# A Gated DeltaNet head's output norm moved out of its recurrence, one head later

## The chip, the cores and the metric

The kernel runs on one core of a Trainium2 chip. The core has a matrix engine (TensorE, PE in the rows), a vector engine (VectorE, DVE), an activation engine (ScalarE, ACT), GpSimd (POOL) and a sync engine (SP), which here issues the DMA transfers. Each engine runs its own list of instructions in order; semaphores tie the lists together. The metric is device time in microseconds (us) of one execution, the median over runs.

## The reference

One decoder block: half a SwiGLU feed-forward step (FFN1), then two mixers side by side (gated linear attention, GLA, and Gated DeltaNet with 8 heads), their gated merge, a second feed-forward step (FFN2) and a final norm. Sequence 1024, model width 1024, float32. The change sits in the Gated DeltaNet heads, whose core is

```python
def gated_delta_attention(q, k, v, g, beta):      # chunks of 64, heads of 128
    ...
    kk = jnp.einsum("bhnid,bhnjd->bhnij", k_beta, k) * decay
    M = jnp.eye(CHUNK, dtype=f32) + jnp.where(strict, kk, 0.0)
    sol = lax.linalg.triangular_solve(M, rhs, left_side=True, lower=True, unit_diagonal=True)
    ...
    def step(S, xs):                               # the recurrence over chunks
        qdc, qkc, uc, wc, kc, gc = xs
        v_new = uc - jnp.einsum("bhcd,bhdv->bhcv", wc, S)
        o = jnp.einsum("bhcd,bhdv->bhcv", qdc, S) + jnp.einsum("bhij,bhjv->bhiv", qkc, v_new)
        S = S * gc[..., None, None] + jnp.einsum("bhcd,bhcv->bhdv", kc, v_new)
        return S, o

def head_rms_norm(o, w, heads):                    # the norm that the change moves
    oh = o.reshape(b, t, heads, -1)
    oh = oh * lax.rsqrt(jnp.mean(oh * oh, axis=-1, keepdims=True) + EPS) * w.astype(jnp.float32)
```

## The kernel before, in words

The time runs through FFN1 (until about 735 us), the eight delta heads (735 to 1395), GLA (to about 1880), the output product, and FFN2. The order of instructions on each engine is not written out by hand. The program is emitted head by head; when it is built, a scheduler places every instruction on its engine's list by its own estimate of when inputs and buffers are ready, so a change in one place can move others. On the chip each list then runs strictly in that order.

One turn `i` of the loop over heads (L1236 and below) emits parts of three heads: the preparation of head `i+1` (`delta_prep`), V projection, levels and recurrence of head `i` (`delta_v`, `delta_levels`, `delta_rec`), and K and Q projections of head `i+2`. All projections are the L138 matmuls: a float32 weight is brought by DMA into `raw` (L112), cast to `wh` by ACT (L119) and its rest taken as `wl` by DVE (L120); these two stand in a scheduler priority block, which lets them be placed far ahead of the code around them. `raw` has two buffers.

`delta_prep` of the next head: transposes of K on PE (L876, into two PSUM banks), squares on ACT (L880, tiles `jk`) and products on DVE (L882) that read those two banks, a Newton iteration for the row norms on DVE (L884 to L889), q·k and k·k products on PE (L902, four banks, each read by DVE in L904 and, with the Newton result, in L908). The result `em` goes to DRAM (`l_d`, L914) and back in another layout (`lt`, L917). POOL then inverts it in 31 steps (L924, L927), and SP writes the inverse to DRAM (`x_d`, L932 and L933, eight transfers) and reads it back (`xb`, `yb`, L944 and L945). The levels (L981, L994 on PE with copies L985, L995 on ACT and subtractions L987, L989, L996 on DVE) finish the inverse `yi`, and the recurrence (PE L1014, L1018, L1022, L1024, L1027; DVE L1016, L1020, L1032) uses it. The loop over heads is therefore also a loop through DMA and POOL: a preparation must pass through `l_d`, `lt`, the inversion and `x_d` before the next head's levels.

The recurrence collects 512 columns of output in a PSUM bank `qo`. The pool of these banks (`bank()`) has four. After each half the norm follows at once: ACT squares `qo` (L1037), DVE adds (L1038), PE sums over the partitions with a matrix of ones (L800, into another bank), ACT takes Ln (L802) and Exp (L803), each with a load of its table, and a square (L804), DVE L805 (which reads the sum's bank), L806, and L1040, which reads `qo`. The two banks stay taken until L805 and L1040.

Of the kernel before, what the change touches and what calls it, by code (L numbers as in the profile page):

```python
# [10 lines left out]
AF = mybir.ActivationFunctionType  # L11
ALU = mybir.AluOpType
# [3 lines left out]
P = 128  # L16
# [5 lines left out]
EPS = 1e-6  # L22
# [16 lines left out]
ORDER = (0, 2, 4, 6, 1, 3, 5, 7)  # L39
# [697 lines left out]
def mixer(st, sto, tc, pool, start, xs, load_unit, dense, ptile, bank, rsqrt_newton, split, new_x, accumulate,  # L737
          ounits, dram, pr, ident, ones, cst, eye, wlr, win, wout, y_d, h_d, sqrt_table, strassen_products, wp, psum, divide, recent, pinned, run):
    nc = tc.nc
# [9 lines left out]
    def big(tag, bufs=None, shape=None):  # L749
        p = cur[0] if cur else me if tag in early else mb  # L750
        return p.tile(shape or [P, T], F32, name=tag, tag=tag, bufs=bufs)
# [8 lines left out]
    def v3(t, n=NCH):  # L760
        return t.rearrange("p (n i) -> p n i", n=n)

    ph = mp.tile([P, 99], F32, name="ph")
# [12 lines left out]
    def half():  # L776
        return sp.tile([P, 512], F32, name="h", tag="h", bufs=4)
# [20 lines left out]
    def out_rms(sq):  # L798
        q = bank()
        nc.tensor.matmul(out=q, lhsT=ones, rhs=sq, start=True, stop=True)  # L800
        t, y = half(), half()
        nc.scalar.activation(out=t, in_=q, func=AF.Ln)  # L802
        nc.scalar.activation(out=y, in_=t, func=AF.Exp, scale=-0.5)  # L803
        nc.scalar.activation(out=t, in_=y, func=AF.Square)  # L804
        nc.vector.scalar_tensor_tensor(out=t, in0=q, scalar=-0.5, in1=t, op0=ALU.mult, op1=ALU.mult)  # L805
        nc.vector.scalar_tensor_tensor(out=y, in0=t, scalar=1.5, in1=y, op0=ALU.add, op1=ALU.mult)  # L806
        return y
# [13 lines left out]
    def delta_kq(i, a, kq=None, steps=None):  # L821
        h = ORDER[i]
        kq = kq or big(f"kq{i % 3}", 1, [P, NCH, 2, P])

        def put(a):
            def f(hf, acc, sg):
                nc.vector.scalar_tensor_tensor(out=kq[:, hf * 4:hf * 4 + 4, a, :], in0=q4(sg), scalar=1.0,
                                               in1=q4(acc), op0=ALU.add, op1=ALU.mult)
            return f

        if a:
            conv_silu(U_DQ + h, h * 4, put(1))
        else:
            conv_silu(U_DK + h, (8 + h) * 4, put(0), (6,), steps)
        return kq

    def delta_decay(i):
        h = ORDER[i]
        gb = big("gb", 2)
        nc.sync.dma_start(out=gb, in_=g_d[h:h + 1, :].broadcast_to([P, T]))  # L840
        gb4 = gb.rearrange("p (n a i) -> p n a i", n=NCH, a=2)
        gla, glb = gb4[:, :, 0, 63], gb4[:, :, 1, 63]
        db = sp.tile([P, NCH, 2], F32, name="db", tag="db", bufs=2)
        nc.vector.tensor_copy(out=db, in_=ngt[:, h, :].unsqueeze(2).broadcast_to([P, NCH, 2]))
        nc.vector.tensor_add(out=db[0:64, :, 1], in0=db[0:64, :, 1], in1=gla[0:64])
        kdec = sp.tile([P, NCH], F32, name="kdec", tag="kdec", bufs=2)
        nc.vector.tensor_add(out=kdec, in0=db[:, :, 1], in1=glb)
        nc.scalar.activation(out=kdec, in_=kdec, func=AF.Exp)
        gl = sp.tile([P, NCH], F32, name="glast", tag="glast", bufs=2)
        nc.vector.tensor_add(out=gl, in0=gla, in1=glb)  # L850
        nc.scalar.activation(out=gl, in_=gl, func=AF.Exp)
        em = big("em", 1)
        nc.vector.tensor_tensor(out=em.rearrange("p (m i) -> p m i", i=64),
                                in0=gb.rearrange("p (m i) -> p m i", i=64),
                                in1=db.rearrange("p n a -> p (n a)").unsqueeze(2).broadcast_to([P, 16, 64]),
                                op=ALU.add)
        nc.vector.tensor_tensor(out=v3(em), in0=v3(em), in1=minmask.unsqueeze(1).broadcast_to([P, NCH, P]),
                                op=ALU.min)
        nc.scalar.activation(out=em, in_=em, func=AF.Exp)
        gla_c = sp.tile([P, NCH], F32, name="glac", tag="glac", bufs=2)  # L860
        nc.vector.tensor_copy(out=gla_c, in_=gla)
        nc.vector.tensor_tensor(out=gb4[:, :, 1, :], in0=gb4[:, :, 1, :],
                                in1=gla_c.unsqueeze(2).broadcast_to([P, NCH, 64]), op=ALU.add)
        nc.scalar.activation(out=gb, in_=gb, func=AF.Exp)

        return gb, gl, kdec, em
# [133 lines left out]
    def delta_rec(kq, qsq, vt3, gl, kst, qk, cj, yi):  # L1000
        kT, qT = kq[:, :, 0, :], kq[:, :, 1, :]
        yi3, kst3, qk3 = v3(yi), v3(kst), v3(qk)
        S = None
        oT = big("oT", 3)
        for b in range(2):
            qo = bank()
            for n in range(4):
                c = b * 4 + n
                rw = sp.tile([P, 256], F32, name="rw", tag="Sg", bufs=2)
                if S is None:  # L1010
                    r = vt3[:, c, :]
                else:
                    q = bank()
                    nc.tensor.matmul(out=q[:, :P], lhsT=kT[:, c, :], rhs=S, start=True, stop=True)  # L1014
                    r = rw[:, :P]
                    nc.vector.tensor_sub(out=r, in0=vt3[:, c, :], in1=q[:, :P])  # L1016
                q = bank()
                nc.tensor.matmul(out=q[:, :P], lhsT=yi3[:, c, :], rhs=r, start=True, stop=True)  # L1018
                w = rw[:, P:]
                nc.vector.tensor_scalar(out=w, in0=q[:, :P], scalar1=cj[:, c:c + 1], scalar2=None, op0=ALU.mult)  # L1020
                oc = qo[:, n * P:(n + 1) * P]
                nc.tensor.matmul(out=oc, lhsT=w, rhs=qk3[:, c, :], start=True, stop=(S is None))  # L1022
                if S is not None:
                    nc.tensor.matmul(out=oc, lhsT=S, rhs=qT[:, c, :], start=False, stop=True)  # L1024
                if c < NCH - 1:
                    q = bank()
                    nc.tensor.matmul(out=q[:, :P], lhsT=kst3[:, c, :], rhs=w, start=True, stop=True)  # L1027
                    s2 = sp.tile([P, P], F32, name="S", tag="S", bufs=2)
                    if S is None:
                        nc.vector.tensor_copy(out=s2, in_=q[:, :P])  # L1030
                    else:
                        nc.vector.scalar_tensor_tensor(out=s2, in0=S, scalar=gl[:, c:c + 1], in1=q[:, :P],  # L1032
                                                       op0=ALU.mult, op1=ALU.add)
                    S = s2
            cc = slice(b * 512, b * 512 + 512)
            osq = half()
            nc.scalar.activation(out=osq, in_=qo, func=AF.Square, scale=P ** -0.5)  # L1037
            nc.vector.scalar_tensor_tensor(out=osq, in0=osq, scalar=EPS * EPS, in1=qsq[:, cc], op0=ALU.add, op1=ALU.add)  # L1038
            fac = out_rms(osq)
            nc.vector.scalar_tensor_tensor(out=oT[:, cc], in0=qo, scalar=ph[:, 98:99], in1=fac,  # L1040
                                           op0=ALU.mult, op1=ALU.mult)
        return oT

    def gla_pre(h):
        la = big("la")
# [179 lines left out]
    for b in range(2):  # L1225
        q = bank()
# [17 lines left out]
    outs = []  # L1244
    for i in range(8):
        kq, (x_d, kst, qk, cj, rs), gl0 = kqs[i], preps[i], gl
        gb0 = gb
        prep = None
        if i < 7:
            gb, gl, kdec, em = nd  # L1250
            prep = delta_prep(i + 1, kqs[i + 1], kdec, em, preps)
            next(prep)
        v = delta_v(i, kq, gb0, rs, vs, prep)
        next(v)
        if i < 6:
            kqs.append(delta_kq(i + 2, 0, None, v))
        else:
            run(v)
        qsq, vt3 = vs[i]
        yi = delta_levels()  # L1260
        if i < 7:
            delta_blocks(em, preps[i + 1][0])
        else:
            stl.close()
            stl = ExitStack()
            mx = pool(stl, "mx")
        outs.append(delta_rec(kq, qsq, vt3, gl0, kst, qk, cj, yi))
        if i < 6:
            delta_kq(i + 2, 1, kqs[i + 2])
            nd = delta_decay(i + 2)  # L1270
        for j in GATES[i]:
            gate(U_DG + ORDER[j], U_MB + ORDER[j], outs[j])
            nc.sync.dma_start(out=y_d[ORDER[j]], in_=outs[j])
        if i < 4:
            nc.sync.dma_start(out=y_d[ORDER[i]], in_=outs[i])
    sums_own, sums_inplace, strassen = strassen_products(
        mx, xs, lambda: wp.tile([P, 512], F32, name="raw", tag="raw", bufs=2),
        lambda: wp.tile([P, 512], F32, name="raw", tag="raw", bufs=2),
# [34 lines left out]
    for g in range(4):  # L1313
# [11 lines left out]
        for a in range(2):  # L1325
            t = 2 * g + a
# [119 lines left out]
```

## Time and profile before

| | |
|---|---|
| median of 3 runs | 2673.62 us (2673.43 to 2679.89) |
| the profiled execution | 2679.65 us, its span 2677.9 us |
| PE busy, granted clock | 94%, mean 0.977 of full |
| DVE, ACT, POOL busy | 70%, 40%, 40% |

The profile is of one execution, 6 us above the median. Times in rows count from the start of its span; an entry in brackets at a row's end is the time that the engine had been idle before that instruction, and what released it.

### The profile page before, as it was taken

The numbers are of one execution on the slowest core, as the hardware profiler recorded it, in microseconds if no ns is written. First come the engines' busy times: TensorE is split into PE (matmuls) and PEld (weight loads), VectorE is DVE, ScalarE is ACT, GpSimd is POOL, SyncE is SP. The second block draws the span as 40 slices with busy tenths as digits, with TensorE's granted clock in tenths as the row PEclk, the third lists the DMA queues.
The fourth block names the chain that finished last, engine by engine and source line by source line (L and its number), as shares of the span: only waits on it lengthen the run. The fifth ranks groups of instructions, "written<-read, shape, count | busy, mean of one in ns | idle before, by whom it ended". The sixth has DMA issues, their size and how long they took to land.

```text
span 2677.9 us, 32736 instructions
## 1 busy us (share of the span) xinstructions
PE 2511.8 (94%) x11656; PEld 2026.9 (76%) x11656; DVE 1868.0 (70%) x2907; ACT 1066.6 (40%) x1845; POOL 1073.0 (40%) x1136
## 2 busy tenths in 40 slices
PE   7899999899997998889989999999989999998998
PEld 6788888677776777767767787877768888886677
DVE  8755556998686777766586766767586555558995
ACT  5333334333352444443344544535233333343331
POOL 5544443653336344343352212221144444346531
PEclk9999999999998999999999999999999999999999
DMA  3222221322221222222211212122312222213222
GB/s 113 79 77 78 84 89 59 115 82 87 95 89 40 64 60 60 60 48 52 64 50 41 80 44 79 48 75 88 121 32 75 68 90 84 87 60 114 79 87 79
DMA packets 150820, 199.05 MB, mean 74 GB/s; under 512 B 69977, under 2 KB 76889, under 8 KB 150657
## 3 DMA queue, kind: packets, MB, share of 16 engines
q1 hardware_dynamic: 146192, 186.14, 22.5%
q0 software_dynamic: 2304, 8.39, 0.8%
q10 hardware_dynamic: 2160, 2.43, 0.3%
q8 instruction: 92, 1.51, 0.2%
q14 instruction: 72, 0.58, 0.1%
HBM read 158.73 MB, written 38.17 MB: 74 GB/s over the span
## 4 chain that ended last, share of the span: by engine, by line
PE 60%; DVE 15%; POOL 10%; issue 5%; ACT 4%; DMA 4%; SPq 2%; POOLq 0%; DVEq 0%; ACTq 0%
PE q L367 28%; PE ps L138 9%; PE m L367 9%; PE q L573 7%; POOL xp L927 4%; POOL itmp L924 4%; DVE wl L126 2%; PE q L902 1%; DVE xl L126 1%; DMA s<-a_d 1%; DVE ha L578 1%; DMA raw<-in_win 1%; DVE h L578 1%; DMA lt<-l_d 1%; SPq L933 1%
## 5 line engine op out<-in xcount | busy, mean ns | idle before, releaser
L126 DVE TENSOR_TENSOR wl<-raw,wh 128x512 fp32r<-128x512 f32 x244 | 201.1, 824 | 172.0 <-ACT wh L125 170.5
L138 PE MATMUL ps<-xl,wh 128*128 128x512 f32 (+2 forms) x736 | 256.9, 408 | 19.9 <-ACT wh L119 8.0
L126 DVE TENSOR_TENSOR wl<-sr,wh 128x512 fp32r<-128x512 f32 x232 | 201.7, 870 | 78.8 <-ACT wh L125 78.4
L138 PE MATMUL ps<-xh,wh 128*128 128x512 f32 (+2 forms) x736 | 255.4, 407 | 0.0
L138 PE MATMUL ps<-xh,wl 128*128 128x512 f32 (+2 forms) x736 | 254.5, 404 | 0.1
L367 PE MATMUL q<-xh,wl 128*128 128x512 f32 x640 | 249.4, 390 | 0.0
L367 PE MATMUL q<-xh,wh 128*128 128x512 f32 x640 | 249.3, 390 | 0.0
L367 PE MATMUL q<-xl,wh 128*128 128x512 f32 x640 | 249.2, 389 | 0.0
L125 ACT CAST wh<-sr 128x512 fp32r<-128x512 f32 x232 | 143.7, 620 | 243.8 <-PE q L573 61.8
L924 POOL TENSOR_TENSOR itmp<-lt,xp 128x112 f32<-128x112 f32 (+29 forms) x248 | 112.0, 451 | 294.1 <-DMA lt<-l_d 275.2
L125 ACT CAST wh<-raw 128x512 fp32r<-128x512 f32 x244 | 145.0, 594 | 175.3 <-PE q L367 100.5
L472 POOL TENSOR_TENSOR s<-s,ysc 128x512 f32<-128x512 f32 x80 | 112.4, 1416 | 247.9 <-ACT s L471 247.9
L138 PEld LDWEIGHTS ps<-xl,wh 128*128 128x128 f32 (+1 forms) x736 | 138.3, 192 | 51.2 <-DVE xl L238 9.1
L355 POOL TENSOR_TENSOR raw<-sr 128x512 f32<-128x512 f32 x20 | 26.4, 1319 | 331.1 <-DMA sr<-in_win 247.8
L138 PEld LDWEIGHTS ps<-xh,wl 128*128 128x128 f32 (+1 forms) x736 | 138.6, 192 | 24.5 <-issue 1.0
L138 PEld LDWEIGHTS ps<-xh,wh 128*128 128x128 f32 (+1 forms) x736 | 138.1, 192 | 24.4 <-issue 1.0
L378 DVE TENSOR_TENSOR c<-c,q 128x512 f32<-128x512 f32 x120 | 82.5, 687 | 84.8 <-PE q L367 84.6
L367 PEld LDWEIGHTS q<-xl,wh 128*128 128x128 f32 x640 | 120.2, 188 | 26.2
L367 PEld LDWEIGHTS q<-xh,wl 128*128 128x128 f32 x640 | 120.1, 188 | 25.6
L367 PEld LDWEIGHTS q<-xh,wh 128*128 128x128 f32 x640 | 120.1, 188 | 25.3
L373 ACT COPY c<-q 128x512 f32<-128x512 f32 x120 | 70.4, 587 | 162.2 <-PE q L367 161.7
L927 POOL TENSOR_TENSOR xp<-xp,itmp 128x112 f32<-128x112 f32 (+29 forms) x248 | 123.0, 496 | 19.4
(481 smaller groups left out, 6752.6 us busy)
## 6 DMA issues: line engine op xcount, KB each, us to landing
sr<-in_win SPq DMA_DIRECT2D x80, 256.0 KB, 2.6
a_d<-s SPq DMA_DIRECT2D x36, 512.0 KB, 3.7
raw<-in_win SPq DMA_DIRECT2D x66, 256.0 KB, 2.7
raw<-in_d SPq DMA_DIRECT2D x56, 256.0 KB, 2.7
raw<-in_g SPq DMA_DIRECT2D x48, 256.0 KB, 2.6
s<-a_d SPq DMA_DIRECT2D x24, 512.0 KB, 4.2
sr<-in_u SPq DMA_DIRECT2D x44, 256.0 KB, 2.7
raw<-in_u SPq DMA_DIRECT2D x44, 256.0 KB, 2.6
```

The lines of the kernel that those rows point to most:

```text
L125: a = nc.scalar.copy(out=hi, in_=src)
L126: b = (eng or nc.vector).tensor_sub(out=lo, in0=src, in1=hi.bitcast(F32))
L138: mm = nc.tensor.matmul(out=ps[:m, sl], lhsT=w[:, :m], rhs=x[:, sl], start=(i == 0 and a == 0), stop=(i == n - 1 and a == 2))
L367: nc.tensor.matmul(out=ps, lhsT=p[:, c], rhs=q, start=(first and k == 0 and a == 0), stop=(k == 3 and a == 2), skip_group_check=not first)
L373: marks[0] = nc.scalar.copy(out=t, in_=ps).ins
L378: marks[1] = nc.vector.tensor_add(out=t, in0=t, in1=ps).ins
L472: nc.gpsimd.tensor_mul(out=s, in0=s, in1=y)
L573: nc.tensor.matmul(out=ps, lhsT=p[:, c], rhs=q, start=(first and k == 0 and a == 0), stop=(k == 1 and a == 2), skip_group_check=not first)
L578: nc.vector.scalar_tensor_tensor(out=hd[:, sl], in0=ps, scalar=0.5, in1=hd[:, sl], op0=ALU.mult, op1=ALU.add)
L902: nc.tensor.matmul(out=q[:, n * 256:n * 256 + 256], lhsT=kT[:, c, :], rhs=kq[:, c, :, :], start=True, stop=True)
L924: inv_eng.tensor_tensor(out=tv, in0=lp[:, j, j + 1:].unsqueeze(2).broadcast_to([P, r, m]), in1=xp[:, j, :m].unsqueeze(1).broadcast_to([P, ...
L927: inv_eng.tensor_tensor(out=xv, in0=xv, in1=tv, op=ALU.subtract)
```

## The change

`delta_rec` no longer normalises. For each half ACT squares `qo` as before and then copies it, scaled, into `oT`, so `qo` is read by ACT alone; DVE's addition goes into a tile `osq` that holds the whole head. A new function `delta_norm` does the rest for the whole head. It is called in the next turn of the loop, after the V projection of the next head has been emitted (for the last head also right after its recurrence). It copies the sums from PSUM to SBUF first, does one Ln and one Exp of 1024 columns in place of two of 512 each, and ends with a multiplication into `oT`. The write of `oT` to `y_d` for the first four heads moves along into the next turn. A smaller scratch for DMA descriptors makes room for the two buffers of `osq` and for `oy`.

```diff
@@ -1002,6 +1002,7 @@
         oT = big("oT", 3)
+        osq = big("osq", 2)
@@ -1033,13 +1034,28 @@
             cc = slice(b * 512, b * 512 + 512)
-            osq = half()
-            nc.scalar.activation(out=osq, in_=qo, func=AF.Square, scale=P ** -0.5)
-            nc.vector.scalar_tensor_tensor(out=osq, in0=osq, scalar=EPS * EPS, in1=qsq[:, cc], op0=ALU.add, op1=ALU.add)
-            fac = out_rms(osq)
-            nc.vector.scalar_tensor_tensor(out=oT[:, cc], in0=qo, scalar=ph[:, 98:99], in1=fac,
-                                           op0=ALU.mult, op1=ALU.mult)
-        return oT
+            sq = osq[:, cc]
+            nc.scalar.activation(out=sq, in_=qo, func=AF.Square, scale=P ** -0.5)
+            nc.scalar.activation(out=oT[:, cc], in_=qo, func=AF.Copy, scale=ph[:, 98:99])
+            nc.vector.scalar_tensor_tensor(out=sq, in0=sq, scalar=EPS * EPS, in1=qsq[:, cc], op0=ALU.add, op1=ALU.add)
+        return oT, osq
+
+    def delta_norm(oT, osq):
+        for b in range(2):
+            cc = slice(b * 512, b * 512 + 512)
+            q = bank()
+            nc.tensor.matmul(out=q, lhsT=ones, rhs=osq[:, cc], start=True, stop=True)
+            nc.vector.tensor_copy(out=osq[:, cc], in_=q)
+        y = big("oy", 1)
+        nc.scalar.activation(out=y, in_=osq, func=AF.Ln)
+        nc.scalar.activation(out=y, in_=y, func=AF.Exp, scale=-0.5)
+        for b in range(2):
+            cc = slice(b * 512, b * 512 + 512)
+            t = half()
+            nc.scalar.activation(out=t, in_=y[:, cc], func=AF.Square)
+            nc.vector.scalar_tensor_tensor(out=t, in0=osq[:, cc], scalar=-0.5, in1=t, op0=ALU.mult, op1=ALU.mult)
+            nc.vector.scalar_tensor_tensor(out=t, in0=t, scalar=1.5, in1=y[:, cc], op0=ALU.add, op1=ALU.mult)
+            nc.vector.tensor_mul(out=oT[:, cc], in0=oT[:, cc], in1=t)
@@ -1252,6 +1268,10 @@
         next(v)
+        if i:
+            delta_norm(*last)
+            if i < 5:
+                nc.sync.dma_start(out=y_d[ORDER[i - 1]], in_=last[0])
@@ -1264,15 +1284,16 @@
-        outs.append(delta_rec(kq, qsq, vt3, gl0, kst, qk, cj, yi))
+        last = delta_rec(kq, qsq, vt3, gl0, kst, qk, cj, yi)
+        outs.append(last[0])
...
+        if i == 7:
+            delta_norm(*last)
...
-        if i < 4:
-            nc.sync.dma_start(out=y_d[ORDER[i]], in_=outs[i])
@@ -1432,7 +1453,7 @@
-    nc = _bacc.Bacc("TRN2", target_bir_lowering=False, num_devices=1)
+    nc = _bacc.Bacc("TRN2", target_bir_lowering=False, num_devices=1, dynamic_dma_scratch_size=2048)
```

Line numbers of the new kernel run one higher inside `delta_rec` (L1014 becomes L1015, L1016 L1017, L1020 L1021, L1022 L1023, L1024 L1025, L1027 L1028, L1032 L1033); its L1038 to L1040 are the square, the copy and the addition, and L1047 to L1058 is `delta_norm`.

The order on PE at the end of a middle head's recurrence, before (L800 is the norm's second sum, L876 the next head's transposes, L902 its products):

```order
L800 MATMUL q<-h,cs 128x512
L876 MATMUL q<-cs,kq_8572 128x128 x8
L138 MATMUL ps<-xh_5413,wl 128x512
L138 MATMUL ps<-xh_5413,wh 128x512 x2
L138 MATMUL ps<-xl_5419,wh 128x512 x2
L138 MATMUL ps<-xh_5418,wl 128x512 x2
L138 MATMUL ps<-xh_5418,wh 128x512 x2
L138 MATMUL ps<-xl_5424,wh 128x512 x2
L138 MATMUL ps<-xh_5423,wl 128x512 x2
L138 MATMUL ps<-xh_5423,wh 128x512 x2
L138 MATMUL ps<-xl_5429,wh 128x512
L902 MATMUL q<-kq_8572 128x256 x4
```

And after, at the same place:

```order
L1019 MATMUL q<-rw,yi 128x128
L876 MATMUL q<-cs,kq_8572 128x128 x5
L1023 MATMUL q<-qk_7671,rw 128x128
L1025 MATMUL q<-kq_7248,S 128x128
L876 MATMUL q<-cs,kq_8572 128x128 x3
L902 MATMUL q<-kq_8572 128x256 x2
L138 MATMUL ps<-xh_5448,wh 128x512
L902 MATMUL q<-kq_8572 128x256 x2
L138 MATMUL ps<-xl_5414,wh 128x512 x2
L138 MATMUL ps<-xh_5413,wl 128x512 x2
L138 MATMUL ps<-xh_5413,wh 128x512 x2
L902 MATMUL q<-kq_8572 128x256 x2
```

The L876 and the first L902 now stand around the recurrence's last two matmuls, with no sum of the norm ahead of them; the two sums (L1047) come 30 L138 matmuls behind the first L902, straight before the next head's L963.

The order on SP is the same in both kernels at the place where the inverse is written: the transfer of a weight tile stands directly behind the eight of `x_d` (before it is `raw_9685`, after `raw_9660`). After:

```order
L932 DMA x_d1_8397<-xp_8407 1024x1x8
L933 DMA x_d1_8397<-xt_8522 32x256
L112 DMA raw_9660<-in_win 128x512
L944 DMA xb_5771<-x_d1_8397 32x8x32
L945 DMA yb_5772<-x_d1_8397 32x8x32
```

What moved is where DVE takes this weight tile apart (L120). Before, at the end of the same recurrence (numbers are those of buffers):

```order
L1016 TENSOR_TENSOR rw_8848<-vt_8354,q_8849 128x128
L850 TENSOR_TENSOR glast_8955<-gb_8947 128x8
L791 SCALAR_TENSOR_TENSOR acc_9226<-ps_9017,ph_5767,acc_9226 128x512
L1020 TENSOR_SCALAR rw_8848<-q_8852,cj_7687 128x128
L862 TENSOR_TENSOR gb_8947<-gb_8947,glac_8962 128x8x64
L954 SCALAR_TENSOR_TENSOR acc_9226<-sig_9231,acc_9226 128x512
L1038 SCALAR_TENSOR_TENSOR h_8857<-h_8857,qsq_8640 128x512
L120 TENSOR_TENSOR wl_9688<-raw_9685,wh_9687 128x512
L968 TENSOR_TENSOR kq1_7910<-kq1_7910,gb_8285 128x1792
```

After:

```order
L120 TENSOR_TENSOR wl_9663<-raw_9660,wh_9662 128x512
L1021 TENSOR_SCALAR rw_8813<-q_8817,cj_7667 128x128
L791 SCALAR_TENSOR_TENSOR acc_9206<-ps_8997,ph_5767,acc_9206 128x512
L1033 SCALAR_TENSOR_TENSOR S_8824<-S_8811,glast_7612,q_8822 128x128
L954 SCALAR_TENSOR_TENSOR acc_9206<-sig_9211,acc_9206 128x512
L1017 TENSOR_TENSOR rw_8826<-vt_8334,q_8827 128x128
L1021 TENSOR_SCALAR rw_8826<-q_8830,cj_7667 128x128
L1033 SCALAR_TENSOR_TENSOR S_8837<-S_8824,glast_7612,q_8835 128x128
L850 TENSOR_TENSOR glast_8936<-gb_8928 128x8
L862 TENSOR_TENSOR gb_8928<-gb_8928,glac_8943 128x8x64
L1017 TENSOR_TENSOR rw_8839<-vt_8334,q_8840 128x128
L1021 TENSOR_SCALAR rw_8839<-q_8843,cj_7667 128x128
```

Before, the L120 of that tile stands behind the recurrence's last DVE instruction (L1020) and the norm's addition (L1038). After, it stands ahead of three of the recurrence's L1021, that is two and a half of its eight steps before its end; the addition (now L1040) comes right below the rows shown. This holds for five of the eight recurrences, the second to the sixth.

## Rows read from the trace of the kernel before

**Rows 1.** The chain that ended last, shares of the span.

```profile
PE 60%; DVE 15%; POOL 10%; issue 5%; ACT 4%; DMA 4%; SPq 2%; POOLq 0%; DVEq 0%; ACTq 0%
```

**Rows 2.** Waits of PE, 750 to 1400 us: total us, times, longest.

```profile
PE q L902 <- DVE h L805: 31.6, 5, 8.9
...
PE q L981 <- DMA xb<-x_d: 13.5, 1, 13.5
...
PE q L1090 <- DVE c L378: 4.0, 1, 4.0
```

**Rows 3.** Timeline of PE, one head: start us, us, instruction.

```profile
1080.03 0.40 PE L1022 MATMUL q<-qk,rw 128*128 128x128 f32 x2
...
1084.17 0.39 PE L1024 MATMUL q<-kq,S 128*128 128x128 f32 x2
...
1091.44 0.61 PE L138 MATMUL ps<-xh,wh 128*128 128x512 f32 x2
...
1091.89 0.39 PE L138 MATMUL ps<-xl,wh 128*128 128x512 f32 x1
...
1099.03 3.78 PE L902 MATMUL q<-kq 128*128 128x256 f32 x8 [6.75 <-DVE h L805]
...
1154.66 0.39 PE L1024 MATMUL q<-kq,S 128*128 128x128 f32 x2
```

**Rows 4.** Timeline of SP's DMA issues, the same head.

```profile
1083.07 0.56 SPq L932 DMA_DIRECT2D x_d<-xp  x1
...
1088.31 0.37 SPq L112 DMA_DIRECT2D raw<-in_win  x1
...
1111.04 1.80 SPq L914 DMA_DIRECT2D l_d<-em  x4
...
1116.30 1.71 SPq L917 DMA_DIRECT2D lt<-l_d  x4
...
1154.75 0.56 SPq L932 DMA_DIRECT2D x_d<-xp  x1
```

**Rows 5.** Timeline of ACT, the same head.

```profile
1091.80 0.62 ACT L119 CAST wh<-raw 128x512 fp32r<-128x512 f32 x1 [6.05 <-DMA raw<-in_win]
...
1092.32 1.05 ACT L967 ACTIVATE qsq<-kq 128x1024 f32<-128x1024 f32 x1
...
1098.54 0.28 ACT L880 ACTIVATE jk<-q 128x128 f32<-128x128 f32 x1
...
1098.94 0.28 ACT L880 ACTIVATE jk<-q 128x128 f32<-128x128 f32 x1
```

**Rows 6.** Timeline of DVE, the same head.

```profile
1079.80 0.68 DVE L120 TENSOR_TENSOR wl<-raw,wh 128x512 fp32r<-128x512 f32 x1
...
1093.41 2.03 DVE L968 TENSOR_TENSOR kq<-kq,gb 128x1792 f32<-128x1792 f32 x1 [0.27 <-ACT qsq L967]
...
1098.29 0.69 DVE L805 SCALAR_TENSOR_TENSOR h<-q,h 128x512 f32<-128x512 f32 x1 [2.85 <-ACT h L804]
...
1102.74 0.16 DVE L884 TENSOR_SCALAR ssk<-ssk 128x8 f32<-128x8 f32 x1
...
1108.85 2.16 DVE L908 SCALAR_TENSOR_TENSOR em<-q,cj,em 128x128 f32<-128x128 f32 x8
```

**Rows 7.** Timeline of POOL, the same head.

```profile
1079.78 0.83 POOL L927 TENSOR_TENSOR xp<-xp,itmp 128x40 f32<-128x40 f32 x1
...
1081.01 0.25 POOL L927 TENSOR_TENSOR xp<-xp,itmp 128x32 f32<-128x32 f32 x1
...
1120.45 0.54 POOL L924 TENSOR_TENSOR itmp<-lt,xp 128x31 f32<-128x31 f32 x1 [36.68 <-DMA lt<-l_d]
```

**Rows 8.** SP's first issue of `x_d`, two other heads.

```profile
946.11 0.57 SPq L932 DMA_DIRECT2D x_d<-xp  x1
...
1224.92 0.56 SPq L932 DMA_DIRECT2D x_d<-xp  x1
```

## The prediction

> **What bounds the kernel now.** The chain that ended last is 60% PE over the whole span [rows 1], so I went to the one stage that the change touches and asked what PE waits for there. Between 750 and 1400 us one wait stands out: L902, the next head's products, behind L805, the norm's step that gives back a PSUM bank: 31.6 us in five waits, 8.9 the longest [rows 2]. The timeline of one head shows how it comes about. The recurrence's last matmul ends at 1084.6; PE has L138 matmuls until 1092.3, then stands still for 6.75 us until 1099.03 [rows 3]. L805 started at 1098.29 [rows 6].
>
> That is the reading which suggests the change. But why is L805 so late? ACT had been idle for 6.05 us until 1091.80, waiting for a weight tile (`raw`), and only behind its cast (L119) come the norm's Ln and Exp [rows 5]. The tile's transfer was issued at 1088.31, directly behind the eight of `x_d`, which began at 1083.07 when POOL's inversion was done [rows 4]. So the wait closes a loop: inversion done → `x_d` → `raw` → ACT and DVE → L902 → L908 → `l_d`, `lt` → next inversion. Its length in this head, from `x_d` to the next `x_d`, is 1154.75 − 1083.07 = 71.7 us [rows 4]; from the second to the sixth of these issues it is (1224.92 − 946.11)/4 = 69.7 [rows 8]. PE by itself needs less: from recurrence end to recurrence end (1084.6 to 1155.05) 70.5, less the wait of 6.75 and about 2 us in which the first matmuls after it ran slowly (eight L902 in 3.78) [rows 3], about 62. **The head's period is set by this loop, not by PE.** Whatever the change does to the wait at L902, the question is whether it makes the loop shorter.
>
> **The change, part by part.** Call X the first issue of `x_d` and T the recurrence's end.
>
> *Taken away.* The bank is free as soon as ACT has squared and copied it, some 1.4 us after T, instead of 14 us after it. The wait at L902 for L805 goes: up to 31.6 us, and some 2 us of slow matmuls behind each. Per head two table loads go and two copies come on ACT, and two copies (0.69 each, like L805 [rows 6]) come on DVE. ACT and DVE have room for these; they matter only by their place.
>
> *Moved.* The order shows that the weight tile issued behind `x_d` is now taken apart on DVE (L120) ahead of three of the recurrence's L1021, in five recurrences; before, it stood behind the whole recurrence. DVE runs in order, so the last two and a half steps now wait for a transfer that cannot start before `x_d`. PE's L1023 waits with them, then T, and behind T everything of the next preparation.
>
> The loop through this place, in the durations of the head shown:
> - X to the cast: 1091.80 − 1083.07 = 8.7 [rows 4, 5]. The queue in front of the tile is the same in both orders.
> - cast 0.62 and L120 0.68 [rows 5, 6]: 1.3.
> - the rest of the recurrence: one step and one more pair of passes took 4.1 (L1022 at 1080.03 to L1024 at 1084.17 [rows 3]). Two steps and the last passes are 7.4 (with fewer L138 between, as the new order has) to 8.6; I take 8.
> - T to the end of L908. ACT: square and copy 1.2, two L880 at 0.4 (1098.54 to 1098.94), L967 1.05, a cast 0.62, four more L880 1.6 [rows 5]. On DVE L968 takes 2.03 and comes behind that cast and its L120; then L882 about 0.69 [rows 6]: done 7.3 after T. From L884 to L908 it was 6.1 (1102.74 to 1108.85 [rows 6]), part of it waiting for the slow L902; I take 4. L908 2.16. Sum 13.3 (12 to 15).
> - L908's end to the next X: 1154.75 − 1111.01 = 43.7 [rows 4, 6]; `l_d`, `lt` and the inversion from 1120.45 [rows 7]. Nothing in it changes.
>
> Sum 8.7 + 1.3 + 8 + 13.3 + 43.7 = 75.0, against 71.7 for the same head. Before, the recurrence's end and the tile's arrival ran side by side; now they stand one behind the other, and what the early bank gives is less than that. PE would reach the same T in about 65 (62, and some 3 for levels that wait for the norm's DVE work, eight steps of 0.69 which now stand ahead of L987), so it waits some 10 us in each of these recurrences. Per head +3.4 (1 to 5.5). Four periods lie between the second and the sixth recurrence's ends: **+13.6** (+4 to +22).
>
> *First head.* The order has 19 more L138 passes ahead of the first head's L902; two passes take 0.45 (1091.44 to 1091.89 [rows 3]), so 4.3 us. What follows is uncovered: PE waits 13.5 us for `xb` there [rows 2]. **+4** (0 to 7). Between the first and second recurrence's ends the order has 176 passes where there were 160, 3.6 us of PE work: **+4** (0 to 5).
>
> *After the sixth recurrence.* One wait at L902 (about 5) goes, the seventh recurrence's tile stands near its end, and about 3 us of L138 work is already done: **−4** (−8 to 0).
>
> *Last head.* Its norm can only follow its recurrence, now with both halves together: two copies (0.69 each) and wider Ln and Exp stand ahead of the gate. PE already waits 4.0 there, at L1090 [rows 2]. **+3** (0 to 5).
>
> *Costed at nothing:* the moved `y_d` transfer (it stands behind `lt` and far ahead of the next `x_d`; without that distance it would add one issue, about 0.5, to the loop); the smaller descriptor scratch itself.
>
> Sum: 13.6 + 4 + 4 − 4 + 3 = +20.6. The profiled execution, 2679.65, would become about 2700; it lies 6.0 above the median, so the median of 2673.62 becomes **2694 us**.
>
> **A rule weighed.** While DVE ran an L120 (1079.80, 0.68), a POOL step of 128x40 took 0.83; the next, 128x32, with DVE elsewhere, 0.25 [rows 6, 7]. The Trainium skill, page "SBUF — State Buffer", section "SBUF: two separate sides", says that a DVE instruction with two SBUF inputs and a GpSimd instruction that reads SBUF shut each other out for a whole instruction; by that rule the trace agrees, since L120 has two. The new norm has eight such instructions per head where the old had four.
>
> **The rivals.**
> - *The plain reading: faster.* The wait at L902 goes and nothing takes its place, because POOL's inversion runs ahead and the tile is there when DVE wants it. Then PE's 65 us decide: 4 × (65 − 69.7) = −19, with the other terms −12, **2662 us** (2649 if the levels don't wait either, at 62). For it: 31.6 us of waits really go. Against it: the loop of 75. It decides if that loop is under 65, that is if X comes 10 us earlier against the recurrence than the pieces above allow. Chance 0.15.
> - *Nothing gained or lost in the loop.* The pieces that I took from one head are 3 us too long (T to L908 at its lower bound, the recurrence's rest at 7.4, the arrival half a microsecond sooner): period 69.7 as before, and only the ends count: 4 + 4 − 4 + 3 = +7, **2681 us**. For it: the same head's loop before was 2 us above the mean. Chance 0.17.
> - *POOL held up by the norm.* Four more DVE instructions per head, each able to add 0.83 − 0.25 = 0.58 to the inversion: 2.3 per head, five inversions, +11.5 on the forecast, **2705 us**. Against it: the norm would be over before the inversion starts, 9.4 us after L908's end (1111.01 to 1120.45 [rows 6, 7]). Chance 0.06. This is what the page's rule above would do here.
> - *The forecast*, slower: chance 0.62, by itself 2682 to 2706.
>
> **How the numbers follow.** A measurement of this kernel can tell about 0.3%, 8 us, from no change. Slower by more than that: nearly all of the forecast and the POOL rival, 0.66. Within it: most of the no-loss rival and the forecast's lower edge, 0.19. Faster: the plain reading, 0.15. The range from 2660 to 2710 takes in the likeliest case and the centres of all the rivals.
>
> **What would show it.** In the changed kernel's profile: L902 no longer waits for the norm. DVE's L120, or ACT's L119, waits for `raw` in the midst of a recurrence, with PE's L1023 waiting for L1021 by 8 to 12 us in each of five heads. The distance from `x_d` to `x_d` in the middle heads is 73 to 75, not 69.7. Smaller waits stand at L981 and L994 in the levels (L985 behind the norm's Exp, L987 behind its DVE steps). The first inversion starts about 4 us later. The prediction is wrong if L1023's waits are small and the period is below 69: then the tile was in time. It is wrong in size if the period is right and the ends are not.

## The result and the profile after

The changed kernel takes **2716.99 us** (median of 4 runs, 2711.33 to 2718.18); the kernel before, run beside it, 2674.2. The ratio is 1.0143, 95% interval 1.0128 to 1.0158: 1.4% slower. That is the predicted side and above the range, whose upper end was 2710. The profiled execution has a span of 2716.4 us where the one of before had 2677.9, so the trace has 38.5 us to account for, of which the prediction's sum had 20.6. The profiled execution of after lies only 1.2 us above its median, that of before 6.0 above the median that the prediction used; the prediction took 6.0 for both, which puts its median another 4.9 us too low.

What PE waits for after, 750 to 1400 us (the view of [rows 2]: total us, times, longest):

```profile
PE q L1023 <- DVE rw L1021: 25.7, 7, 5.4
PE q L981 <- DMA xb<-x_d: 13.3, 1, 13.3
PE q L981 <- ACT h L985: 10.4, 4, 2.6
PE q L1015 <- DVE S L1033: 8.1, 3, 5.1
PE q L994 <- DVE h L987: 6.2, 6, 1.7
...
PE q L1047 <- DVE em L908: 2.4, 1, 2.4
```

The wait at L902 for the norm is gone, as it was bound to be. In its place PE waits inside the recurrence, at L1023 and L1015. The twelve largest groups of waits in this stretch add up to 76.9 us, and before to 70.4, so waits alone don't tell why the kernel is 38 us slower.

One middle head, SP's issues (as [rows 4]):

```profile
1099.40 0.56 SPq L932 DMA_DIRECT2D x_d<-xp  x1
...
1104.91 0.37 SPq L112 DMA_DIRECT2D raw<-in_win  x1
...
1174.76 0.56 SPq L932 DMA_DIRECT2D x_d<-xp  x1
```

ACT in the same head (as [rows 5]); the last row is the copy that L981 waits for, behind the norm's Exp:

```profile
1108.18 0.62 ACT L119 CAST wh<-raw 128x512 fp32r<-128x512 f32 x1 [5.77 <-DMA raw<-in_win]
...
1136.30 1.06 ACT L1051 ACTIVATE oy<-oy 128x1024 f32<-128x1024 f32 x1
...
1139.53 0.57 ACT L985 COPY h<-q 128x512 f32<-128x512 f32 x1
```

DVE (as [rows 6]):

```profile
1108.83 0.69 DVE L120 TENSOR_TENSOR wl<-raw,wh 128x512 fp32r<-128x512 f32 x1 [4.25 <-ACT wh L119]
1109.44 0.34 DVE L1021 TENSOR_SCALAR rw<-q,cj 128x128 f32<-128x128 f32 x1
...
1128.76 2.14 DVE L908 SCALAR_TENSOR_TENSOR em<-q,cj,em 128x128 f32<-128x128 f32 x8
```

And PE (as [rows 3]):

```profile
1105.48 0.40 PE L138 MATMUL ps<-xl,wh 128*128 128x512 f32 x1
1109.84 0.49 PE L1023 MATMUL q<-qk,rw 128*128 128x128 f32 x2 [3.96 <-DVE rw L1021]
...
1110.85 1.04 PE L138 MATMUL ps<-xh,wl 128*128 128x512 f32 x2
...
1118.39 0.39 PE L1025 MATMUL q<-kq,S 128*128 128x128 f32 x2
```

Read across the four engines, this is the predicted chain: `x_d` at 1099.40, the tile's issue behind it at 1104.91, ACT's cast at 1108.18 after 5.77 us of waiting for the tile, DVE's L120, and only then the L1021 that PE's L1023 wants. The recurrence ends at 1118.8, 19.4 us after `x_d`; before, the two lay 1.5 us apart [rows 3, 4]. The distance from `x_d` to `x_d` is 75.4 us in this head. For the mean over four heads, the first issues of the third and the seventh head (as [rows 8]; the prediction calls them the second and the sixth, after the recurrences that they stand beside):

```profile
948.21 0.56 SPq L932 DMA_DIRECT2D x_d<-xp  x1
...
1250.44 0.56 SPq L932 DMA_DIRECT2D x_d<-xp  x1
```

(1250.44 − 948.21)/4 = 75.6, against 69.7 before [rows 8]. Every mean distance below is taken over these same four periods.

Why do the waits look so small? Busy time and granted clock of the same head in pieces cut at the rows above (columns: stretch; its length; busy time and count of PE, its weight loads, DVE, ACT, POOL; PEclk, the granted clock as a share of full; DMA share; GB/s):

```profile
1099.40:1105.80 6.40, 6.40 (x36) 5.15 (x34) 4.48 (x10) 1.54 (x3) 1.13 (x1) 1.00 0.36 41
1105.80:1109.84 4.04, 0.08 (x2) 0.00 (x1) 1.01 (x3) 0.62 (x1) 0.00 (x0) 1.00 0.57 111
1109.84:1114.70 4.86, 4.86 (x19) 4.18 (x20) 2.26 (x5) 0.63 (x1) 0.00 (x0) 0.65 0.55 156
...
1130.90:1174.76 43.86, 40.07 (x214) 32.97 (x213) 34.26 (x60) 17.59 (x26) 29.56 (x62) 0.88 0.13 40
```

PE stands still for 4 us, and in the 4.86 us behind that stop the mean granted clock is 0.65 of full, between its two levels (1.2 and 2.4 GHz). In the last piece, which holds a second stop of 2.6 us at L981, it is 0.88. Over four whole periods, recurrence end to recurrence end, after and then before:

```profile
967.88:1268.46 300.58, 263.91 (x1337) 214.71 (x1335) 207.99 (x442) 108.75 (x213) 121.88 (x252) 0.89 0.20 51
```

```profile
948.90:1227.64 278.74, 248.24 (x1338) 200.52 (x1337) 201.93 (x434) 116.76 (x220) 123.23 (x252) 0.94 0.22 55
```

Of the 21.8 us that these periods grew, 15.7 stand as busy time of PE with the same number of matmuls, and 6.2 as idle time. 248.24 × 0.94/0.89 = 262, so the lower clock makes up nearly all of the former. Part of a stall thus shows as slow matmuls, and a table of waits shows too little of it.

### The profile page after: what moved, and what is told of

Its sections match the earlier page's. It is cut to its first block, busy times and chain, and to the rows that moved or that the text cites. A ratio compares the mean times of both kernels' runs of the same rounds, so it can differ in the third digit from the quotient of the medians.

```text
span 2716.4 us, 32749 instructions
## 1 busy us (share of the span) xinstructions
PE 2530.6 (93%) x11656; PEld 2044.6 (75%) x11656; DVE 1879.8 (69%) x2923; ACT 1054.2 (39%) x1831; POOL 1072.2 (39%) x1136
## 4 chain that ended last, share of the span: by engine, by line
PE 62%; DVE 15%; POOL 10%; issue 5%; ACT 3%; DMA 3%; SPq 2%; DVEq 0%; POOLq 0%; ACTq 0%
PE q L367 28%; PE ps L138 11%; PE m L367 10%; PE q L573 6%; POOL xp L927 4%; POOL itmp L924 4%; DVE wl L126 2%; DVE xl L126 1%; DVE ha L578 1%; DVE h L578 1%; DMA lt<-l_d 1%; DVE xl L238 1%; PE q L902 1%; DMA raw<-in_win 1%; DVE wl L120 1%
## 5 line engine op out<-in xcount | busy, mean ns | idle before, releaser
L138 PE MATMUL ps<-xl,wh 128*128 128x512 f32 (+2 forms) x736 | 266.3, 419 | 24.0 <-DVE xl L238 14.6
L138 PE MATMUL ps<-xh,wh 128*128 128x512 f32 (+2 forms) x736 | 256.8, 410 | 0.0
L138 PE MATMUL ps<-xh,wl 128*128 128x512 f32 (+2 forms) x736 | 256.3, 410 | 0.1
L125 ACT CAST wh<-raw 128x512 fp32r<-128x512 f32 x244 | 144.9, 594 | 177.2 <-PE q L367 98.3
L138 PEld LDWEIGHTS ps<-xl,wh 128*128 128x128 f32 (+1 forms) x736 | 142.4, 198 | 55.9 <-DVE xl L238 9.2
L138 PEld LDWEIGHTS ps<-xh,wl 128*128 128x128 f32 (+1 forms) x736 | 142.4, 197 | 25.0 <-issue 1.1
L138 PEld LDWEIGHTS ps<-xh,wh 128*128 128x128 f32 (+1 forms) x736 | 141.6, 196 | 25.9 <-issue 0.6
L119 ACT CAST wh<-raw 128x512 fp32r<-128x512 f32 x94 | 58.1, 619 | 208.1 <-PE ps L138 141.6
L927 POOL TENSOR_TENSOR xp<-xp,itmp 128x112 f32<-128x112 f32 (+29 forms) x248 | 127.6, 514 | 19.4
```

Source lines behind the costliest of these rows:

```text
L119: nc.scalar.copy(out=wh, in_=raw)
L125: a = nc.scalar.copy(out=hi, in_=src)
L138: mm = nc.tensor.matmul(out=ps[:m, sl], lhsT=w[:, :m], rhs=x[:, sl], start=(i == 0 and a == 0), stop=(i == n - 1 and a == 2))
L927: inv_eng.tensor_tensor(out=xv, in0=xv, in1=tv, op=ALU.subtract)
```

## The experiments

Ten kernels were run. The theory: one weight tile, whose transfer stands behind `x_d`, is taken apart inside the recurrence. The trace shows this in five recurrences, as the order had it, but in the sixth the tile's L120 is ahead of two of the L1021, not three. The main rivals: the smaller descriptor scratch; the norm's place one head later; its steps on ACT and DVE in the levels. "Before" is run beside each kernel again.

**The scratch alone**, in the kernel before:

```diff
-    nc = _bacc.Bacc("TRN2", target_bir_lowering=False, num_devices=1)
+    nc = _bacc.Bacc("TRN2", target_bir_lowering=False, num_devices=1, dynamic_dma_scratch_size=2048)
```

> The kernel before with the smaller descriptor scratch alone. The scratch theory: it shifts instructions at the start of the program and at the hand-over to the delta heads, so the first inversion starts late by about 10 us of the 10.3 seen in the changed kernel, the loop over heads stays at about 70 us and L902 goes on waiting for L805 by about 30 us; total 4 to 10 us above before. The rival, that the late first head comes from the moved norm: no difference from before within 3 us.

2682.7 us, ratio 1.0018 (1.0006 to 1.0031). The first `x_d` comes at 831.65; before it was 822.28 (first row below the scratch alone, second row the kernel before):

```profile
831.65 0.69 SPq L932 DMA_DIRECT2D x_d<-xp  x1
```

```profile
822.28 0.68 SPq L932 DMA_DIRECT2D x_d<-xp  x1
```

After, it is 832.44. So the late first head is due to the scratch, which I had costed at nothing; by the medians some 5 us of it are left at the end. The loop's mean is 69.0 us and L902 waits 29.1 us for L805: the scratch does not explain the longer loop.

**A third buffer for `raw`**, in the changed kernel; it lets the transfer start before `x_d` and leaves the rest of the code; the scheduler places some instructions otherwise:

```diff
-            raw = stage() if stage else wp.tile([P, 512], F32, name="raw", tag="raw", bufs=2)
+            raw = stage() if stage else wp.tile([P, 512], F32, name="raw", tag="raw", bufs=3)
```

> The changed kernel with a third buffer for weight tiles. In its order the tile behind x_d is taken apart after the recurrence. The wait theory (the recurrence waits for a tile queued behind x_d): PE's waits L1023 and L1015 fall from 38 us to under 12, x_d to x_d falls from 75.6 to 66 to 70 us, total 2675 to 2692 us. The rival, that the norm's work one head later is what costs (levels, ACT and DVE queues): waits move elsewhere, x_d to x_d stays above 73, total above 2705.

2672.49 us, ratio 0.9989 (0.9977 to 1.0000): 0.0154 or some 41 us less than the changed kernel, and the loss is gone. The total lies 2.5 us below the expected span. The distance from `x_d` to `x_d` falls to 67.9, inside it. In the fourth recurrence, the one shown above, DVE's list still has an L120 at the same place, ahead of the last three L1021; its `x_d` begins at 1085.81, and now L120 finds its tile there:

```profile
1088.75 0.29 DVE L1017 TENSOR_TENSOR rw<-vt,q 128x128 f32<-128x128 f32 x1
1088.96 0.68 DVE L120 TENSOR_TENSOR wl<-raw,wh 128x512 fp32r<-128x512 f32 x1
1089.67 0.35 DVE L1021 TENSOR_SCALAR rw<-q,cj 128x128 f32<-128x128 f32 x1
```

So the place does harm only together with a late transfer. What PE waits for, 740 to 1430 us:

```profile
PE q L981 <- DMA xb<-x_d: 13.4, 1, 13.4
PE q L981 <- ACT h L985: 8.7, 4, 2.6
PE m L367 <- ACT c L373: 8.7, 2, 6.2
PE q L994 <- DVE h L987: 6.8, 5, 2.2
```

L1023's waits are down to 1.7 us in all; those of the levels (L981 for L985, L994) are about as they were, 8.7 and 6.8 us after 10.4 and 6.2. The chain that ended last shows the same, after and then with three buffers:

```profile
PE 62%; DVE 15%; POOL 10%; issue 5%; ACT 3%; DMA 3%; SPq 2%; DVEq 0%; POOLq 0%; ACTq 0%
```

```profile
PE 71%; DVE 13%; ACT 4%; issue 3%; POOL 3%; DMA 2%; SPq 0%; DVEq 0%; POOLq 0%; ACTq 0%
```

With two buffers POOL's inversion is part of the chain (10%, as in [rows 1]); with three it is nearly off it (3%). The theory held.

**The head weights on ACT's DMA queue**, in the changed kernel, two buffers:

```diff
-            nc.sync.dma_start(out=raw, in_=src[:, hf * 512:hf * 512 + 512])
+            load_unit.q.dma_start(out=raw, in_=src[:, hf * 512:hf * 512 + 512])
...
+    load_unit.q = nc.scalar
```

> The changed kernel with the weight tiles of the eight heads issued from ACT's DMA queue, so that none stands behind x_d. The wait theory: the wait of L119 for raw (37 us) and that of L1023 (28 us) go, x_d to x_d 64 to 69 us, total 2665 to 2690. The rival (norm one head later): above 2705.

2711.2 us, ratio 1.0128 (1.0108 to 1.0149), `x_d` to `x_d` 76.5: a miss. The tile stayed tied to `x_d`, and now it held up ACT's whole list (line numbers of the recurrence are 2 higher in this kernel, so L1040 is the square, L1019 the subtraction ahead of L1021's matmul; ACT, then DVE, then PE):

```profile
1106.18 0.34 ACTq L112 DMA_DIRECT2D raw<-in_win  x1
1106.56 0.60 ACT L1040 ACTIVATE osq<-q 128x512 f32<-128x512 f32 x1 [12.76 <-DMA x_d<-xp]
```

```profile
1107.19 0.69 DVE L1042 SCALAR_TENSOR_TENSOR osq<-osq,qsq 128x512 f32<-128x512 f32 x1 [9.66 <-ACT osq L1040]
```

```profile
1108.13 0.80 PE L1021 MATMUL q<-rw,yi 128*128 128x128 f32 x2 [9.36 <-DVE rw L1019]
```

ACT stood still until the tile's issue at 1106.18; by the profile a transfer of `x_d` ended that stop, with which the issue shares no data. What ties the two is not shown; no run tried it.

**The norm at hand**, straight behind its recurrence, otherwise as changed:

```diff
-        if i:
-            delta_norm(*last)
...
+        delta_norm(*last)
```

> The changed kernel with the norm of a whole head called straight after its recurrence, not one head later; all else kept (sums copied out of PSUM, one Ln and Exp of 1024). In its order the tile behind x_d is taken apart after the recurrence, as before. The wait theory: no wait of L1023 over 3 us, x_d to x_d 68 to 72, total 2675 to 2690. The rival, that the copies and wider steps themselves cost: above 2700.

2688.82 us, ratio 1.0043 (1.0029 to 1.0057); `x_d` to `x_d` 70.3, both as expected. The order puts the tile's L120 behind the recurrence again, L1023 waits 2.6 us in all, and most of the loss is gone without a third buffer. The norm's place and the tile's place change together here, so this run alone does not part them.

**A third buffer in the kernel before** (with the smaller scratch, to make room), the counterpart of the second experiment:

> The kernel before with the smaller scratch and a third buffer for weight tiles; the norm as before. The tile theory (what sets the period is the tile behind x_d, for the wait at L902 too): L902's wait for L805 falls from 29 us to under 10, x_d to x_d from 70 to 66 to 68 us, total 2652 to 2668. The bank theory (the norm holds the bank, as the change supposes): L902 goes on waiting over 20 us, total 2675 or more.

2678.68 us, ratio 0.9998 (0.9985 to 1.0012); `x_d` to `x_d` 69.1. ACT no longer waits for a tile, but L902 still waits for the norm:

```profile
PE q L902 <- DVE oT L1040: 22.5, 4, 6.9
PE q L981 <- DMA xb<-x_d: 13.5, 1, 13.5
PE q L902 <- DVE h L805: 7.6, 6, 1.4
```

This is what the bank theory had said, and with it a part of my reading of before fell: the tile is not the only reason for the wait at L902. With the tile in time the same 30 us are waited for the banks that the norm holds.

**The same with a scratch of 14336**:

> The same with the scratch made smaller by 2 KB only, just enough for the third buffer. If the late first head comes from the instructions that the 2 KB scratch moves, the first x_d comes at 822 as before, and the total is 4 to 9 us below the run before this one; if it comes from the third buffer or the scratch as such, there is no difference.

2673.65 us, ratio 0.9985 (0.9974 to 0.9997); the first `x_d` is at 824.54. The scratch's price is 0.0013 or some 3 us in this pair (5 by the medians), whose intervals overlap.

**The norm at hand and a third buffer:**

> The changed kernel with the norm straight after its own recurrence and a third buffer. The tile theory: x_d to x_d 66 to 68 us, total 2660 to 2674, within 5 us of the changed kernel with three buffers. If one head later is worth something of its own, it is slower than that one by more than 8 us.

2666.74 us, ratio 0.9962 (0.9942 to 0.9981); `x_d` to `x_d` 65.3. Faster than both kernels. It is also some 7 us faster than the changed kernel with three buffers (0.9989), more than the 5 that I allowed, and on the side that speaks against the later place.

**No norm at all**, as a bound (the changed kernel without `delta_norm`: heads go out unnormalised):

> The changed kernel without delta_norm: the heads' outputs stay unnormalised, only the square, the scaled copy and the addition are left; two buffers for weight tiles. In its order the tile behind x_d stands after the recurrence. The tile theory: no wait in the recurrence over 3 us, but the tile still gates the next preparation, x_d to x_d 64 to 69 us, total 2650 to 2678. The rival, that the norm's own work set the changed kernel's period: well under 64 us and 2645.

2640.71 us, ratio 0.9861 (0.9833 to 0.989), `x_d` to `x_d` 64.3. The period is inside the theory's span (64 to 69), but the total is below it and below the 2645 that the rival named, so this run does not decide between them. It could not do so alone: here too the order puts the tile behind the recurrence, so the tile's place changed along with the norm. Beside the third buffer it gives the shares: of the 11.3 us per head between the changed kernel (75.6) and this one, 7.7 go with the norm kept and the tile in time (67.9). Against the kernel before, the norm of eight heads costs 0.0139 or some 37 us.

**The copy first, alone**, in the kernel before, two buffers and the old scratch; the norm stays by halves in the recurrence:

```diff
+            nc.scalar.activation(out=oT[:, cc], in_=qo, func=AF.Copy, scale=ph[:, 98:99])
...
-            nc.vector.scalar_tensor_tensor(out=oT[:, cc], in0=qo, scalar=ph[:, 98:99], in1=fac,
-                                           op0=ALU.mult, op1=ALU.mult)
+            nc.vector.tensor_mul(out=oT[:, cc], in0=oT[:, cc], in1=fac)
```

> The kernel before with one part of the change alone: ScalarE copies qo out of PSUM (with the scale) before the norm, and the last multiply, now from SBUF, is a tensor_mul. The norm stays in the recurrence by halves, two weight tile buffers, old scratch. In its order the weight tile queued behind the x_d writes stands behind the recurrence in all middle heads. If the banks and the tile bind together as the third-buffer run on the kernel before says (either alone frees little), L902's 30 us of waits shrink but the tile's wait of about 7 us per head stays: 2668 to 2680. If the banks alone set L902's wait: 25 us less wait, 2650 to 2662. If the copy (four more ScalarE passes on 128x512 per head) delays ScalarE's other work: 2680 to 2690.

2677.56 us, ratio 0.9994 (0.9978 to 1.0009), as the first of the three cases said. L902's waits fall to 16.3 us, and nothing is gained in all: ACT waits 34.1 us for tiles (before 37.3, 740 to 1430 us). In two points the expectation was wrong. The copy adds two ScalarE passes per head, not four. And in one of the heads the tile stands inside the recurrence, between two of its L1020 (DVE's rows there):

```profile
1012.13 0.35 DVE L1020 TENSOR_SCALAR rw<-q,cj 128x128 f32<-128x128 f32 x1
1022.85 0.69 DVE L120 TENSOR_TENSOR wl<-raw,wh 128x512 fp32r<-128x512 f32 x1 [10.37 <-ACT wh L119]
...
1024.12 0.34 DVE L1032 SCALAR_TENSOR_TENSOR S<-S,glast,q 128x128 f32<-128x128 f32 x1
```

That makes a control within one kernel. SP, ACT and PE in that head:

```profile
1013.59 0.56 SPq L932 DMA_DIRECT2D x_d<-xp  x1
...
1090.79 0.56 SPq L932 DMA_DIRECT2D x_d<-xp  x1
```

```profile
1022.20 0.62 ACT L119 CAST wh<-raw 128x512 fp32r<-128x512 f32 x1 [13.95 <-DMA raw<-in_win]
```

```profile
1024.51 0.80 PE L1014 MATMUL q<-S,kq 128*128 128x128 f32 x2 [9.89 <-DVE S L1032]
```

X to the cast is again 8.6 us, PE waits 9.9 us in the recurrence, and this head's `x_d` to `x_d` is 77.2, while its four neighbours in the loop have 67.6, 69.4, 68.5 and 63.4. The norm had not been moved here: the tile's place, with its late transfer, is enough for the stall.

**The copy first and a third buffer** (smaller scratch):

> The same copy first in the kernel before, with three weight tile buffers and the smaller scratch, so its partner is the third-buffer run on the kernel before (2678.7). If the early release of the banks is what the change is worth once the tile is in time: the wait of L902 on the multiply that reads PSUM (22.5 us there) is gone and the time is 2655 to 2668, like the norm at hand with three buffers (2666.7). If the gain came from norming the whole head at once (fewer, wider steps) and not from the banks: 2674 to 2680.

2663.94 us, ratio 0.9939 (0.9921 to 0.9957), inside the span expected for the banks, `x_d` to `x_d` 65.3, and the fastest with the whole computation. Of the waits at L902 this is left, 740 to 1430 us:

```profile
PE q L902 <- DVE h L805: 7.7, 6, 1.4
```

The kernel before was held by two things, the tile and the banks: the third buffer alone gave 0.9998 (0.9985 with the larger scratch), the copy alone 0.9994, both 0.9939. But the copy's figure has the stalled head in it. That period is 8.7 us longer than the mean of the other three middle ones (68.5); without it, and if none of it is made up later, the copy alone would stand near 0.996 by an estimate from these rows. So that the two bind jointly, each worth nothing without the other, is not shown.

The whole change with a third buffer (0.9989) is slower than the last kernel by 0.0050, some 13 us (2677.06 × 0.0050). About half of this goes with the later place: against the norm of the whole head at hand (0.9962) it loses some 7. The rest, some 6, lies between the whole head at hand and the halves in place. In both of these steps the intervals overlap a little. The early release of the bank is enough for the whole gain; that the wide steps add to it is not shown.

## Why the prediction was right in its mechanism and too small

The mechanism is shown. The tile's place in DVE's list together with its late transfer decides: with the transfer in time the loss goes, though the L120 stands at its place; in one head of a kernel without the moved norm such a place makes a stall of 9.9 us.

**The loop's pieces held.** For the head at 1099.40: X to the cast 8.78 (predicted 8.7); cast and L120 1.34, to 1109.52 (1.3); the rest of the recurrence, to 1118.78, 9.26 (8), with the clock at 0.65 behind the stop; T to L908's end at 1130.90, 12.1 (13.3); from there to the next X 43.86 (43.7). Sum 75.4, predicted 75.0. The closeness of the sum is in part luck: the rest of the recurrence came out 1.3 us longer, T to L908's end 1.2 us shorter. (The prediction's own parts of T to L908's end, 7.3 + 4 + 2.16, make 13.5 and not 13.3.)

**The step that failed: "against 71.7 for the same head … Per head +3.4."** The sum of the new loop was right, but I set it against one head of before, of which I had written myself that it lay 2 us above the mean of 69.7. Four periods have to be compared with four periods. The `x_d` distances grew by 75.6 − 69.7 = 5.9 each; recurrence end to end the four periods grew by 21.8, where the term said +13.6. With 69.7 in its place the predicted sum would have given 4 × 5.3 = +21. The no-loss rival has the same slip: to come from 75.0 to a period of 69.7 the pieces would have to be 5.3 us too long, not 3.

**The second step: "Between the first and second recurrence's ends … +4".** I counted PE's added passes only. But the second recurrence is the first of the five that wait for their tile. Its last L1024 (L1025 after) starts 19.7 us behind its `x_d` (967.88 − 948.21); before it was 2.8 (948.90 − 946.11). That lag of 16.9 is entered once. The `x_d` itself came 5.3 us sooner behind the first recurrence's end than before, and 5.1 of this lie before L908's end. Before, PE had no wait at L902 in this head; it waited at the norm's second sum (L800), whose addition L1038 stood on DVE behind a late tile's L120:

```profile
885.47 1.14 PE L800 MATMUL q<-h,cs 128*128 128x512 f32 x2 [3.86 <-DVE h L1038]
```

Together 16.9 − 5.3 = +11.6.

**The smaller terms.** First head: predicted +4, measured +7.4 at the first recurrence's end. The scratch, "costed at nothing", covers the whole of it, since alone it moves that end by 9.5 (888.67 against 879.14); what the 19 passes cost is not shown. From the sixth recurrence's end to the eighth's: predicted −4, measured −1.2. Last head: predicted +3, measured −1.1. The whole account: 7.4 + 11.6 + 21.8 − 1.2 − 1.1 = 38.5.

**The waits.** Five stalls of 8 to 12 us at L1023 were forecast; the rows show up to 5.4. PE reached the place later than I reckoned, because its matmuls had run slowly behind earlier stops: 15.7 us more busy time over four periods is 3.9 in each. The period was set by the loop all the same, so this changed the picture of the stall and not its price.

**"The head's period is set by this loop, not by PE"** was half the truth of before: with the tile in time the banks held by the norm kept the period at 69.1, which the third buffer in the kernel before showed. For the change this did not matter, since it freed the banks and lengthened the other loop.

The rivals: the plain reading had the tile in time. With a third buffer, where that holds, `x_d` to `x_d` is 67.9, three above the 65 that it reckoned with; its price for the change as such was wrong. POOL held up by the norm: I had said that the norm would be over before the inversion starts. It was not quite. The norm's last two multiplications (DVE, then POOL, the same head):

```profile
1140.47 1.40 DVE L1058 TENSOR_TENSOR oT<-oT,h 128x512 f32<-128x512 f32 x2
```

```profile
1140.72 0.60 POOL L927 TENSOR_TENSOR xp<-xp,itmp 128x31 f32<-128x31 f32 x1
1141.40 0.61 POOL L924 TENSOR_TENSOR itmp<-lt,xp 128x60 f32<-128x60 f32 x1
...
1142.80 0.33 POOL L924 TENSOR_TENSOR itmp<-lt,xp 128x87 f32<-128x87 f32 x1
```

Two steps beside them take 0.60 and 0.61, a larger one a little later 0.33; in the head of before the same two steps took 0.27 and 0.29. That agrees with the Trainium skill, page "SBUF — State Buffer", section "SBUF: two separate sides", by which an instruction with two SBUF inputs on DVE and one of GpSimd that reads SBUF shut each other out. But it is under 1 us of this head, and from L908's end to the next X it is 43.86 as against 43.7, so it lengthened nothing there.

## What to carry to other kernels

When a wait names one releaser, look at what would bind next before crediting its removal: here, with the tile's wait gone, the banks that the norm holds bound next, and the third buffer alone was worth nothing that could be told (0.9998). After any change of order, find the instructions that wait for a late transfer and see what stands behind them in the same engine's list; one 0.7 us instruction in front of a recurrence's step cost about 6 us per head, and one more buffer took that away. Compare the sum of a new loop with the mean over the same periods before, and count the once-only lag when a loop's phases shift.

## What was not expected of the hardware

- Behind a stop of 4 us in the recurrence the mean granted clock over the next 4.86 us was 0.65, and over four periods of the changed kernel it was 0.89 where before it was 0.94 and with three buffers 0.95. Most of what the stall cost is booked as PE's busy time.
- A transfer that was moved from SP's queue to ACT's still came only after `x_d`, and ACT stood idle for 12.76 us around its issue. Another queue did not make it independent here; why is open.
